# A layer of state space and attention: tables stored in eight parts, attention loads held back by the emitter, its clock corrected, and one vector operation exchanged

## The chip, the cores and the metric

One core of a Trainium2 chip. The metric is the device time of one execution in microseconds (us). The kernel before was timed three times: 1916.57, 1918.79 and 1922.06 us, median 1918.79. A separate, profiled execution left the trace that all rows below come from. TensorE is called PE, VectorE DVE, ScalarE ACT, GpSimd POOL, SyncE SP.

## The reference

S = 2048 tokens, D = 1024 channels, one layer, fp32. In short:

```python
mod = silu(c) @ w_ada + b_ada                       # shift | scale | gate
u = layer_norm(h) * (1 + scale) + shift
(x_ssm, z_ssm, q, k, v, f_logit, z_attn, g_ssm, g_attn) = split(u @ w_in)
y_ssm = s5(x_ssm)                # 32 groups of 16 channels, 64 complex states, scan over 2048 tokens, gelu, GLU
y_ssm = (y_ssm * silu(z_ssm)) @ w_proj_ssm
log_f = log_sigmoid(f_logit + b_f)
# 8 heads of 64: causal softmax(q k / 8 + cum_f[t] - cum_f[j]) @ v
y_attn = (o * silu(z_attn)) @ w_proj_attn
merged = sigmoid(g_ssm) * y_ssm + sigmoid(g_attn) * y_attn
h = layer_norm(ALPHA * h + (merged @ w_out) * gate, ln_g, ln_b)
```

## The kernel before, in words

**Products.** Each fp32 matrix is split into a high and a low part, and a product is the sum of three matmuls (high·high, low·high, high·low). A tile of the input projection (`pp` in the rows) is 8 times three matmuls of 128x512 in one of four PSUM banks. `uh`/`ul` are the parts of the modulated input, `hi`/`lo` those of the weights, loaded as `raw` and split on POOL.

**Stages in order of time.** The modulation sums `acc` over eight chunks of `w_ada` on DVE, and PE sums them over partitions (`bg<-ident,acc`, with `pr` for the keys' weights); x is normalized on DVE and transposed on PE (`pt<-ident,xt`); the projection follows, whose results go through `st` to scratch in HBM (`x_sc`, `zs_sc`, `q_sc`, `k_sc`, `ga_sc`, ...). Beside it, DVE computes the state-space tables `pk` (128 x 32 groups x 163 numbers), which SP writes to `pk_sc`. The 32 state-space groups come next, still beside projection tiles: `stage_l` (L988) loads `pkg` (one group's table) and `xr`, POOL builds `G` and others, DVE builds `CA`, and `bg<-CA,pkg` is the first matmul of a group. Then attention: 64 rounds (8 heads, 8 pairs of query blocks) of scores (`sc<-ks,qd`), exponentials (`srow`), their transposes (`pt<-ident,srow`) and products with v (`acc`), with the GLU and the two projections (`bg<-bh,wh` and the like) put between. `ks`, `fb`, `vs` are a chunk of 512 keys, biases and values; `qd` the queries of two rounds. `lb` is four divided by a row's sum of exponentials, spread over 64 columns, which PE transposes (`acc<-ident,lb`). The output projection and the last layer norm end the program.

**Order of the work.** Nothing reorders instructions on the chip. `Model` (L42) is a rough clock: `cost` (L99) gives each instruction's duration, `deps` (L80) when its operands are there. `merge` (L168) takes streams in order of rank and emits the next step of the first one that would not wait at the model's PE time; so the numbers in `cost` decide what stands where on every engine. `Engine` calls go through L209, which is why nearly all rows say L209. `sp.dma_start` puts a transfer into SP's single queue at once; `sp.later` (L223) holds it until the model says that its operands are there. SP works in order: a transfer that waits holds up those behind it. The two merges are at L663 (start) and L1760 (the rest). `pools` (L1230) opens the room of attention in two steps, `at["p"]` when the state space is done, `atp` when the projection is done; a ring of six chunks has two places in the first and four in the second.

The lines that matter most:

```python
# L105, cost, PE
return max(n, 2) * (0.4167 if n >= 256 else 1.667)
# L963, ssm_params
sp.dma_start(out=pk_sc.rearrange("g p n -> p g n"), in_=pk)
# L1583, exponentials
dve.tensor_scalar(out=lb, in0=li.to_broadcast([128, 2, 64]), scalar1=4.0, scalar2=None, op0=ALU.mult)
```

Of the kernel before, what the change touches and what calls it, by code (L numbers as in the profile page):

```python
# [16 lines left out]
S = 2048  # L17
D = 1024
NW = 4          # token windows of 512
WT = 512  # L20
KD = D // 128
NG = 32         # state-space groups
GH = 16         # channels of a group
CL = 8          # tokens of a chunk
NCH = S // CL   # chunks
CW = WT // CL   # chunks of a window
# [10 lines left out]
PKN = 163       # of a group: Bbar 16 | swapped 16 | C 16 | swapped 16 | tables 64 | powers 19 | A^7..A^0 16  # L37
# [4 lines left out]
class Model:  # L42
    """A rough clock of the engines, by which the order of emission is chosen (it computes no data)."""

    # from the end of an instruction to the start, on another engine (or the same), of one that needs it
# [34 lines left out]
    def deps(self, e, kw):  # L80
        """When the operands are there for engine e (whose own accesses are in order)."""
        rd, wt = self.aps(kw)
        r = 0.0
        for n in rd:
            if n in self.wr:
                end, by = self.wr[n]
                r = max(r, end + self.lat(e, by))
            for h in self.held:
                if n in h[2]:           # (a transfer that is still to come)
                    r = max(r, max(h[0] + 1100, self.t["sp"] + 1100, self.t["dma"]) + 1700)  # L90
# [8 lines left out]
    def cost(self, e, op, kw):  # L99
# [4 lines left out]
        if e == "pe":  # L104
            if op == "transpose":  # L105
                return n * 0.835
            if kw["rhs"].dtype == F32R:
                return max(n, 2) * (0.4167 if n >= 256 else 1.667)
            return max(n * 1.667, 60.0)
# [12 lines left out]
        if e == "act":  # L122
            c = (60 if kw["in_"].space == PSUM else 95) + 0.833 * n
            return c + 178 * isinstance(kw.get("scale"), bass.AP) + 90 * ("accum_out" in kw)
        if e == "pool":
            if op == "memset":
# [4 lines left out]
                   and v.space == bass.MemoryType.DRAM and v.ap[-1][0] == 1] + [512])  # L131
        return n * o.shape[0] * 4 / 360.0 * 512 / row

    def run(self, e, op, kw):
        c, r = self.cost(e, op, kw), self.deps(e, kw)
        if e == "sp":
# [3 lines left out]
            end = self.t["dma"] + 1000  # L140
# [5 lines left out]
        for n in wt:  # L146
            # parts of a tile that transfers fill do not wait for each other
# [3 lines left out]
    def settle(self, rd, wt, dma=False):  # L151
        """Emit what is held and has to come before a read of rd and a write of wt (transfers may fill parts of a
        tile in any order)."""
# [14 lines left out]
    def merge(self, streams):  # L168
        """Emit from the first stream whose next step would not wait; streams come in order of rank."""
# [27 lines left out]
class Engine:  # L197
    """An engine whose instructions the model sees."""
# [14 lines left out]
    def when(self, **kw):  # L213
        """When an instruction with these operands could start."""
# [3 lines left out]
    def soon(self, op, /, **kw):  # L218
        """A stream's step: the instruction, emitted once it would not wait."""
# [3 lines left out]
    def later(self, op, /, **kw):  # L223
        """The instruction, emitted once its operands are there (the streams go on meanwhile)."""
# [6 lines left out]
def hybrid_layer(ctx: ExitStack, tc: tile.TileContext, x, c, w_ada, b_ada, w_in, b_f, lam_re, lam_im,  # L231
# [32 lines left out]
    def pround(o, i):  # L264
        """Pool's copy into float32r (its rounding)."""
# [13 lines left out]
    bt = const.tile([128, 24], F32, name="bt")  # L279
    psp = pl(ctx, "psp", space=PSUM)  # L280
# [4 lines left out]
    # maskb[q, k] = 0 where k <= q, NEG elsewhere  # L285
# [4 lines left out]
    # ------------------------------------------------------------------ phase 1: input projection  # L290
    esl = ExitStack()               # left: until the projection is done
# [11 lines left out]
    def ps_tile(n=[0]):  # L303
        """One of four banks, which attention later has for scores (three) and outputs."""
# [7 lines left out]
    def bg_tile(n=None):  # L312
        if n is not None and n % 4 > 1:         # (the banks of the transposes, once attention is done)
            return pt_tile()
# [5 lines left out]
    def bank():  # L320
        """Whichever of the two banks of bg_tile is free."""
# [12 lines left out]
    def split_wide(raw, n):  # L334
        """A stream that splits a chunk of weights; the tiles are there at once."""
# [8 lines left out]
    def rstd_of(p, mv, n):  # L344
        """1 / sqrt(var + eps) of the variances mv[:, :, 1]."""
# [21 lines left out]
    def until(f):  # L367
        """A condition to wait on, whatever the time."""
        return lambda: 0.0 if f() else None

    def modulation():
        """shift | 1 + scale of silu(c) @ w_ada + b_ada, as columns, 128 channels at a time."""
# [3 lines left out]
        act.activation(out=one, in_=ident[:, 0:1], func=AF.Sqrt)    # (its table is there when the layer norm needs it)  # L376
# [43 lines left out]
    def early_keys():  # L420
        """Two column tiles of the keys' weights, with which the first window goes on while the next one comes."""
# [7 lines left out]
    def modulation_columns():  # L429
        """Sums over the partitions, as columns."""  # L430
# [17 lines left out]
    def column_sums(acc, n, c0):  # L448
        """mods[:, c0:] = sums of acc over its partitions, as columns, + b_ada."""
# [34 lines left out]
    def normalized():  # L484
        """Windows of tokens, less their mean and over their spread."""
# [21 lines left out]
    def modulated():  # L507
        """u = normalized * (1 + scale) + shift, channels on partitions."""
# [28 lines left out]
    def low_parts():  # L537
        """The two parts of u."""
# [23 lines left out]
    def products_of(ps, w, hi, lo, c0):  # L562
        """A tile of columns of the projection of a window."""
# [7 lines left out]
    def store_parts(kind, m, w, ps):  # L571
        """Queries (scaled) or keys, in two parts."""
# [92 lines left out]
    # the other columns, with the state-space branch alongside  # L665
# [55 lines left out]
    def forget_bias():  # L721
        """f_sc[h, t] = cumulative log_sigmoid(f + b_f)."""
        with ExitStack() as es:
# [10 lines left out]
            # log1p(e) = 2 artanh(s), s = e / (2 + e) <= 1/3  # L734
# [25 lines left out]
    def gate():  # L760
        """The gate part of the modulation, as a row (scaled by 1/16, which the merge leaves)."""
# [1029 lines left out]
```

## Time and profile before

| | |
|---|---|
| median of three executions | 1918.79 us |
| span of the profiled execution | 1913.3 us |
| PE busy | 1833.8 us (96%), 10104 matmuls |
| DVE busy | 1082.5 us (57%) |
| POOL busy | 923.6 us (48%) |
| ACT busy | 775.1 us (41%) |
| moved by DMA | 252.37 MB, mean 132 GB/s |

The span is the time from the first to the last instruction of the profiled execution; the median execution is 5.5 us longer, which is what lies around the span and the difference between executions. The shares are averages over stages that differ: POOL is busy 48% over the span and 94% in the state-space groups. What a row calls a wait is idle time of an engine, put down to what ended it.

### The profile page before, as it was taken

The numbers are of one execution on the slowest core, as the hardware profiler recorded it, in microseconds if no ns is written. First come the engines' busy times: TensorE is split into PE (matmuls) and PEld (weight loads), VectorE is DVE, ScalarE is ACT, GpSimd is POOL, SyncE is SP. The second block draws the span as 40 slices with busy tenths as digits, with TensorE's granted clock in tenths as the row PEclk, the third lists the DMA queues.
The fourth block names the chain that finished last, engine by engine and source line by source line (L and its number), as shares of the span: only waits on it lengthen the run. The fifth ranks groups of instructions, "written<-read, shape, count | busy, mean of one in ns | idle before, by whom it ended". The sixth has DMA issues, their size and how long they took to land. (4 is left out here: it accounts for less than half of the span.)

```text
span 1913.3 us, 30538 instructions
## 1 busy us (share of the span) xinstructions
PE 1833.8 (96%) x10104; PEld 1565.5 (82%) x10104; DVE 1082.5 (57%) x2886; ACT 775.1 (41%) x1849; POOL 923.6 (48%) x1343
## 2 busy tenths in 40 slices
PE   4999999998999999999998999999999999899997
PEld 3789988886787888888887888988889888788886
DVE  8651114734555555552004777876777866567666
ACT  5441111121433444443114767876767866311110
POOL 5222111113889999995306566376543436533110
PEclk9899999998999999999998999999999999999999
DMA  9434346654333333335217365265364543744432
GB/s 302 138 86 119 94 110 183 149 133 121 101 94 105 100 105 97 105 101 138 91 50 189 98 169 140 77 183 152 113 201 131 151 137 127 260 146 136 131 123 89
DMA packets 276915, 252.37 MB, mean 132 GB/s; under 512 B 66396, under 2 KB 211828, under 8 KB 276756
## 3 DMA queue, kind: packets, MB, share of 16 engines
q1 hardware_dynamic: 276756, 250.41, 45.7%
q8 instruction: 80, 1.31, 0.3%
q14 instruction: 79, 0.65, 0.1%
HBM read 159.50 MB, written 86.63 MB: 129 GB/s over the span
## 5 line engine op out<-in xcount | busy, mean ns | idle before, releaser
L209 PE MATMUL pp<-uh,hi 128*128 128x512 f32 x1136 | 451.0, 397 | 0.0
L209 PE MATMUL pp<-uh,lo 128*128 128x512 f32 x1136 | 446.0, 393 | 0.0
L209 PE MATMUL pp<-ul,hi 128*128 128x512 f32 x1136 | 445.1, 392 | 0.0
L209 ACT ACTIVATE st<-pp 128x512 f32<-128x512 f32 (+2 forms) x168 | 93.9, 559 | 439.1 <-PE pp L209 383.4
L209 DVE TENSOR_TENSOR pl<-pt,ph 128x512 fp32r<-128x512 f32 (+1 forms) x288 | 183.3, 657 | 122.3 <-ACT ph L209 121.7
L209 PEld LDWEIGHTS pp<-uh,lo 128*128 128x128 f32 x1136 | 214.2, 189 | 46.3
L209 PEld LDWEIGHTS pp<-uh,hi 128*128 128x128 f32 x1136 | 216.4, 190 | 41.5
L209 PEld LDWEIGHTS pp<-ul,hi 128*128 128x128 f32 x1136 | 214.7, 189 | 41.9
L209 ACT ACTIVATE srow<-srow,nm 128x512 f32<-128x512 f32 (+2 forms) x320 | 207.6, 653 | 0.4 <-DVE nm L209 0.3
L209 ACT ACTIVATE ph<-pt 128x512 fp32r<-128x512 f32 (+1 forms) x288 | 159.8, 572 | 64.4 <-PE pt L209 51.6
L209 DVE CUSTOM_DVE_ANT_0 srow<-sc,fb 128x512 f32<-128x512 f32 (+3 forms) x288 | 163.0, 594 | 21.9 <-PE sc L209 21.9
L209 PE MATMUL sc<-ks,qd 128*128 128x512 f32 (+2 forms) x640 | 163.7, 381 | 7.1 <-DMA qd<-q_sc 7.1
L209 PE MATMUL pt<-ident,srow 128*128 128x128 f32 x1088 | 159.3, 275 | 8.7 <-DVE pl L209 4.7
L209 PE MATMUL acc<-ph,vs 128*128 128x256 f32 x576 | 163.0, 308 | 2.5 <-POOL ph L209 2.5
L209 POOL TENSOR_TENSOR oo<-oo 64x256 f32<-64x256 f32 x128 | 93.7, 732 | 143.0 <-ACT oo L209 140.0
L209 POOL TENSOR_SCALAR hi<-raw 128x512 fp32r<-128x512 f32 x60 | 39.9, 665 | 237.8 <-PE pp L209 191.7
L209 PEld LDWEIGHTS pt<-ident,srow 128*128 128x128 f32 x1088 | 128.4, 141 | 27.2 <-DVE pl L209 9.5
L209 PE MATMUL acc<-pl,vs 128*128 128x256 f32 x576 | 147.4, 282 | 0.5 <-DVE pl L209 0.5
L209 PE MATMUL bg<-bh,wh 128*128 128x512 f32 (+1 forms) x384 | 140.2, 365 | 5.1 <-DVE zt L209 5.1
L209 PE MATMUL bg<-bh,wl 128*128 128x512 f32 (+1 forms) x384 | 138.1, 360 | 0.0
L209 PE MATMUL bg<-bl,wh 128*128 128x512 f32 (+1 forms) x384 | 137.8, 359 | 0.0
L209 PEld LDWEIGHTS sc<-ks,qd 128*128 128x128 f32 x640 | 107.9, 193 | 24.4 <-issue 8.4
(240 smaller groups left out, 3811.3 us busy)
## 6 DMA issues: line engine op xcount, KB each, us to landing
xt<-in_x_dram SPq DMA_DIRECT2D x32, 512.0 KB, 3.7
qd<-q_sc SPq DMA_DIRECT2D x64, 256.0 KB, 5.4
raw<-in_w_in_dram SPq DMA_DIRECT2D x30, 512.0 KB, 4.5
wada<-in_w_ada_dram SPq DMA_DIRECT2D x16, 512.0 KB, 7.0
k_sc<-st SPq DMA_DIRECT2D x32, 256.0 KB, 3.3
v_sc<-st SPq DMA_DIRECT2D x32, 256.0 KB, 2.3
q_sc<-st SPq DMA_DIRECT2D x16, 512.0 KB, 3.3
gs_sc<-st SPq DMA_DIRECT2D x32, 256.0 KB, 2.3
```

The source lines that it names most:

```text
L209: return fn(kw["out"], 0.0) if op == "memset" else fn(**kw)
```

## The change

- **The clock** (`Model.cost` and `run`): a matmul of 256 columns or more costs 13 ns more; an activation that also sums costs 185 ns for it instead of 90; a transfer's duration follows another formula in the length of its rows; a transfer ends 1600 ns instead of 1000 after its data.
- **The tables**: `pk` is stored in eight transfers of four groups each. `stage_l` loads a group once the clock says that its own part is stored.
- **The attention loads** (`load_keys`, `load_q`) are held back (`sp.later`) instead of being put into SP's queue at once, and `pools` asks for one more `load_q` and two more `load_keys` as soon as `atp` is open.
- **lb**: a product with a constant tile of fours instead of a product with the number 4.

The rest of the diff removes comments. Its core:

```diff
@@ Model.cost, Model.run
-                return max(n, 2) * (0.4167 if n >= 256 else 1.667)
+                return 13 + 0.4167 * n if n >= 256 else max(n, 2) * 1.667
...
-            return c + 178 * isinstance(kw.get("scale"), bass.AP) + 90 * ("accum_out" in kw)
+            return c + 178 * isinstance(kw.get("scale"), bass.AP) + 185 * ("accum_out" in kw)
...
-                   and v.space == bass.MemoryType.DRAM and v.ap[-1][0] == 1] + [512])
-        return n * o.shape[0] * 4 / 360.0 * 512 / row
+                   and v.space == bass.MemoryType.DRAM and v.ap[-1][0] == 1] + [4096])
+        return n * o.shape[0] * 4 / row * (9 + 0.045 * row) / 16
...
-            end = self.t["dma"] + 1000
+            end = self.t["dma"] + 1600
@@ hybrid_layer
+    fours = const.tile([128, 2, 1], F32, name="fours")
...
+    nc.gpsimd.memset(fours, 4.0)
@@ ssm_params, stage_l
             yield sp.when(in_=pk)
-            sp.dma_start(out=pk_sc.rearrange("g p n -> p g n"), in_=pk)
+            for i in range(0, NG, PKG):
+                sp.dma_start(out=pk_sc[i:i + PKG].rearrange("g p n -> p g n"), in_=pk[:, i:i + PKG])
+                sq["stored"].append(M.t["dma"] + 2500)
...
+    PKG = 4
...
-            yield sp.when(out=pk, b=xr)
+            yield max(sp.when(out=pk, b=xr), sq["stored"][g // PKG])
+            M.t["sp"] = max(M.t["sp"], sq["stored"][g // PKG])
             sp.dma_start(out=pk, in_=pk_sc[g])
@@ load_keys, load_q (the other four transfers likewise)
-        sp.dma_start(out=f32(ks), in_=k_sc[h, :, :, tk].rearrange("a d t -> (a d) t"))
+        sp.later("dma_start", out=f32(ks), in_=k_sc[h, :, :, tk].rearrange("a d t -> (a d) t"))
@@ pools
         atp = pl(esat, "atp", side="right")
+        load_q()
+        load_keys()
+        load_keys()
@@ exponentials
-                dve.tensor_scalar(out=lb, in0=li.to_broadcast([128, 2, 64]), scalar1=4.0, scalar2=None, op0=ALU.mult)
+                dve.tensor_mul(out=lb, in0=li.to_broadcast([128, 2, 64]), in1=fours.to_broadcast([128, 2, 64]))
```

What it moves, in the program's own order. PE at the start, from the end of the second of the eight column sums (a sum is two of `bg<-ident,acc` and two of `bg<-ident,pr`) to the first projection matmuls; before:

```order
L209 MATMUL bg<-ident,acc 128x128
L209 MATMUL bg<-ident,pr 128x128
L209 MATMUL pt<-ident,xt 128x128 x8
L209 MATMUL bg<-ident,acc 128x128
L209 MATMUL bg<-ident,pr 128x128
L209 MATMUL bg<-ident,acc 128x128
L209 MATMUL bg<-ident,pr 128x128
L209 MATMUL pp<-uh_0_84,hi 128x512
L209 MATMUL pp<-ul_0_100,hi 128x512
L209 MATMUL pp<-uh_0_84,lo 128x512
L209 MATMUL pp<-uh_0_84,hi 128x512
L209 MATMUL pp<-ul_0_100,hi 128x512
```

Now:

```order
L209 MATMUL bg<-ident,acc 128x128
L209 MATMUL bg<-ident,pr 128x128
L209 MATMUL bg<-ident,acc 128x128
L209 MATMUL bg<-ident,pr 128x128
L209 MATMUL pp<-uh_0_86,hi 128x512
L209 MATMUL pp<-ul_0_102,hi 128x512
L209 MATMUL pp<-uh_0_86,lo 128x512
L209 MATMUL pp<-uh_0_86,hi 128x512
L209 MATMUL pp<-ul_0_102,hi 128x512
L209 MATMUL pp<-uh_0_86,lo 128x512
L209 MATMUL pt<-ident,xt 128x128 x4
L209 MATMUL pp<-uh_0_86,hi 128x512
```

Eight transposes of x stood behind the second sum, and the projection began behind the third. Now four transposes stand ahead of the second sum, and the projection begins behind it. Ahead of the eighth sum stand 22 triples of projection matmuls instead of 12.

SP where the state-space tables are stored (`pk_sc<-pk`) and the first groups loaded (`pkg`, `xr`); before:

```order
L209 DMA zs_sc<-st 128x512 x3
L209 DMA raw<-in_w_in_dram 128x8x128
L209 DMA pk_sc<-pk 128x32x163
L209 DMA dsk<-in_ssm_d_dram 16x32x1
L209 DMA pkg<-pk_sc 128x163
L209 DMA xr<-x_sc 128x256
L209 DMA pkg<-pk_sc 128x163
L209 DMA xr<-x_sc 128x256
L209 DMA zs_sc<-st 128x512 x3
```

Now:

```order
L209 DMA zs_sc<-st 128x512 x2
L209 DMA pk_sc<-pk 128x4x163 x8
L209 DMA dsk<-in_ssm_d_dram 16x32x1
L209 DMA zs_sc<-st 128x512
L209 DMA pkg<-pk_sc 128x163
L209 DMA xr<-x_sc 128x256
L209 DMA pkg<-pk_sc 128x163
L209 DMA xr<-x_sc 128x256
L209 DMA raw<-in_w_in_dram 128x8x128
```

One store became eight, one projection store now stands ahead of the first `pkg`, and a load of weights went from ahead of the tables to behind the second group. On PE the first `bg<-CA,pkg` stands behind 2053 projection matmuls instead of 2083; between the first and the last group stand 1494 instead of 1509.

SP where the projection ends and attention starts; before:

```order
L209 DMA ga_sc<-st 128x512 x13
L209 DMA qd<-q_sc 64x2x512 x2
L209 DMA ks<-k_sc 128x512
L209 DMA fb<-f_sc 128x512
L209 DMA vs<-v_sc 128x4x128
L209 DMA yr<-y_sc 128x8x64 x2
L209 DMA wraw<-in_w_glu_dram 128x4x128 x2
L209 DMA zt<-zs_sc 128x512 x3
L209 DMA qd<-q_sc 64x2x512 x2
```

Now:

```order
L209 DMA ga_sc<-st 128x512 x13
L209 DMA qd<-q_sc 64x2x512 x2
L209 DMA ks<-k_sc 128x512
L209 DMA fb<-f_sc 128x512
L209 DMA vs<-v_sc 128x4x128
L209 DMA ks<-k_sc 128x512
L209 DMA fb<-f_sc 128x512
L209 DMA vs<-v_sc 128x4x128
L209 DMA yr<-y_sc 128x8x64 x2
L209 DMA wraw<-in_w_glu_dram 128x4x128 x2
L209 DMA zt<-zs_sc 128x512 x3
L209 DMA qd<-q_sc 64x2x512 x2
```

A second chunk of keys (`ks`, `fb`, `vs`, 256 KB each) now stands between the first and the second pair of `qd`. At the other end of attention, nine triples of background products instead of six stand behind the last `acc` on PE.

## Rows read from the trace of the kernel before

**Rows 1.** The page: its head and part 1 (busy us, share of span, instructions).
```profile
span 1913.3 us, 30538 instructions
...
PE 1833.8 (96%) x10104; PEld 1565.5 (82%) x10104; DVE 1082.5 (57%) x2886; ACT 775.1 (41%) x1849; POOL 923.6 (48%) x1343
```
**Rows 2.** Stretches: length, busy time of each engine, TensorE's clock, DMA share, GB/s.
```profile
600.00:700.00 100.00, 100.00 (x476) 80.51 (x475) 53.67 (x117) 42.69 (x104) 93.82 (x148) 1.00 0.36 102
1050.00:1600.00 550.00, 532.54 (x3405) 469.02 (x3404) 415.87 (x1365) 394.60 (x994) 295.37 (x458) 0.99 0.49 141
1600.00:1700.00 100.00, 91.06 (x564) 82.34 (x563) 59.95 (x108) 33.44 (x72) 56.12 (x63) 0.97 0.61 200
```
**Rows 3.** Waits of PE: what for, us in total, times, longest.
```profile
PE bg L209 <- DVE acc L209: 13.7, 7, 2.8
...
PE bg L209 <- DVE CA L209: 7.6, 1, 7.6
PE sc L209 <- DMA qd<-q_sc: 7.1, 2, 6.9
PE bg L209 <- DVE zt L209: 5.1, 3, 3.8
...
PE acc L209 <- DVE lb L209: 3.1, 4, 1.4
```
**Rows 4.** Timeline of PE at the first group: start, us, instruction, [idle before].
```profile
459.52 0.39 PE L209 MATMUL pp<-uh,lo 128*128 128x512 f32 x1
467.48 0.61 PE L209 MATMUL bg<-CA,pkg 128*16 128x128 f32 x2 [7.58 <-DVE CA L209]
...
472.14 0.51 PE L209 MATMUL pp<-uh,hi 128*128 128x512 f32 x1
```
**Rows 5.** Timeline of all engines from the last table entry to CA.
```profile
444.33 0.43 DVE L209 TENSOR_TENSOR pk<-ta,ta 128x256 f32<-128x256 f32 x1
...
459.33 0.33 SPq L209 DMA_DIRECT2D pkg<-pk_sc  x1
...
461.29 0.41 POOL L209 TENSOR_TENSOR G<-pkg 128x128 f32<-128x128 f32 x1 [12.48 <-DMA pkg<-pk_sc]
...
464.10 0.60 ACT L209 ACTIVATE st<-pp 128x512 f32<-128x512 f32 x1 [13.08 <-DMA zs_sc<-st]
...
465.34 0.54 DVE L209 SCALAR_TENSOR_TENSOR CA<-pkg,sgn 128x144 f32<-128x144 f32 x1
```
**Rows 6.** The page, part 6: DMA issues, KB each, us to landing.
```profile
ks<-k_sc SPq DMA_DIRECT2D x32, 256.0 KB, 5.9
...
pk_sc<-pk SPq DMA_DIRECT2D x1, 2608.0 KB, 14.5
```
**Rows 7.** Timeline of ACT: two projection tiles in a row (24 matmuls apart).
```profile
434.11 0.60 ACT L209 ACTIVATE st<-pp 128x512 f32<-128x512 f32 x1 [4.84 <-PE pp L209]
439.55 0.60 ACT L209 ACTIVATE st<-pp 128x512 f32<-128x512 f32 x1 [4.84 <-PE pp L209]
```
**Rows 8.** Timeline of SP and PE where attention starts.
```profile
1014.34 1.27 SPq L209 DMA_DIRECT2D qd<-q_sc  x2
...
1026.69 1.26 SPq L209 DMA_DIRECT2D qd<-q_sc  x2
...
1033.67 1.62 PE L209 MATMUL sc<-ks,qd 128*128 128x512 f32 x3 [6.89 <-DMA qd<-q_sc]
```
**Rows 9.** Stretches while tables are stored and where attention starts (columns of rows 2).
```profile
446.00:458.00 12.00, 12.00 (x55) 9.94 (x54) 1.05 (x4) 0.60 (x1) 2.73 (x3) 1.00 1.09 217
...
1026.00:1032.00 6.00, 0.78 (x3) 0.30 (x2) 4.96 (x16) 4.35 (x13) 6.00 (x7) 0.73 0.89 241
```
**Rows 10.** Tile lb: ns min/median/max, first and last start.
```profile
L209 DVE TENSOR_SCALAR lb<-li x64: 226/230/2329, 1018.1 to 1607.8; 128x128 f32<-128x128 f32 x64
```
**Rows 11.** Tile m in the groups, same columns.
```profile
L209 DVE TENSOR_TENSOR m<-bg,cs x32: 405/423/426, 475.0 to 877.9; 128x256 f32<-128x256 f32 x32
...
L209 DVE TENSOR_TENSOR m<-gs,cs x32: 406/662/1341, 479.9 to 880.2; 128x255 f32<-128x255 f32 x32
```
**Rows 12.** Timeline of PE at the eighth column sum.
```profile
53.83 0.63 PE L209 MATMUL pp<-uh,lo 128*128 128x512 f32 x1
55.73 0.76 PE L209 MATMUL bg<-ident,acc 128*128 128x128 f32 x2 [1.27 <-DVE acc L209]
```
**Rows 13.** Timeline of ACT where the second window's products begin.
```profile
81.81 0.60 ACT L209 ACTIVATE st<-pp 128x512 fp32r<-128x512 f32 x1 [4.36 <-DMA x_sc<-st]
```

More of the change, by code (lines that the diff above doesn't have):

```diff
@@ L962, in ssm_params @@
             yield sp.when(in_=pk)
-            sp.dma_start(out=pk_sc.rearrange("g p n -> p g n"), in_=pk)
-    sq = dict(a=0, b=0, c=0, d=0, e=0, r=0, x=0, t=0, ready=False, st={})
+            for i in range(0, NG, PKG):
+                sp.dma_start(out=pk_sc[i:i + PKG].rearrange("g p n -> p g n"), in_=pk[:, i:i + PKG])
+                sq["stored"].append(M.t["dma"] + 2500)
+    PKG = 4
+    sq = dict(stored=[], a=0, b=0, c=0, d=0, e=0, r=0, x=0, t=0, ready=False, st={})
     esss = ExitStack()
@@ L1209, in load_keys @@
         tk = slice(j * 512, (j + 1) * 512)
-        sp.dma_start(out=f32(ks), in_=k_sc[h, :, :, tk].rearrange("a d t -> (a d) t"))
-        sp.dma_start(out=fb, in_=f_sc[h:h + 1, tk].to_broadcast([128, 512]))
-        sp.dma_start(out=f32(vs), in_=v_sc[h, tk, :].rearrange("(n p) e -> p n e", p=128))
+        sp.later("dma_start", out=f32(ks), in_=k_sc[h, :, :, tk].rearrange("a d t -> (a d) t"))
+        sp.later("dma_start", out=fb, in_=f_sc[h:h + 1, tk].to_broadcast([128, 512]))
+        sp.later("dma_start", out=f32(vs), in_=v_sc[h, tk, :].rearrange("(n p) e -> p n e", p=128))
         at["k"][h, j], at["v"][h, j], at["f"][h, j] = ks, vs, fb
@@ L1221, in load_q @@
         for hf in range(2):
-            sp.dma_start(out=f32(qd[hf * 64:(hf + 1) * 64]),
-                         in_=q_sc[:, h * 64:(h + 1) * 64, p_ * 256:(p_ + 2) * 256].rearrange("a d t -> d a t"))
+            sp.later("dma_start", out=f32(qd[hf * 64:(hf + 1) * 64]),
+                     in_=q_sc[:, h * 64:(h + 1) * 64, p_ * 256:(p_ + 2) * 256].rearrange("a d t -> d a t"))
         at["q"][r], at["q"][r + 1] = qd[:, :, 0:256], qd[:, :, 256:512]
```

## The prediction

> **What bounds the kernel now.** I read part 1 of the page first. PE is busy 1833.8 of 1913.3 us [rows 1], so all that any change of order can win is the 79.5 us in which PE stands idle, plus what PE loses by a lower clock after idling. No edit adds or removes a matmul. The second view is the list of PE's waits [rows 3]: the reader is to see that no single wait is large. The sums of the modulation cost 13.7 us in seven waits, the first state-space group 7.6 in one, the second pair of queries 7.1, the merge's operands 5.1, lb 3.1. The third view is the table of stretches [rows 2]: in the state-space groups PE is busy 100.00 of 100.00 us, and POOL beside it 93.82; in attention PE is busy 532.54 of 550, so 17.5 us are idle there, in many short gaps; in the merge 91.06 of 100. So there are four places where the change can win, and one (the groups) where it can only lose.
>
> **The change part by part.** All terms are against the profiled span of 1913.3 us. The median execution, 1918.79, is 5.5 us above that, and I carry these 5.5 us over. A difference below about 0.3% (5.8 us) can't be told from no change here.
>
> *Tables in eight parts.* The last entry of `pk` is written at 444.33 (+0.43), and the store takes 14.5 us to land [rows 5, 6]. SP waits for it, issues the first `pkg` at 459.33, POOL starts on it at 461.29, and PE's first matmul of a group starts at 467.48 after 7.58 us idle [rows 4, 5]. Part of the time behind the landing is not the tables': ACT's `st` at 464.10 waited 13.08 us for a store of projections that stood in SP's queue behind the waiting `pkg`, and DVE's `CA` (465.34) stands behind the `st` of the same tile. After the idle time PE runs at half pitch until 472.14, which costs half of 472.14 − 467.48 = 4.66, so 2.3 us. The place costs 7.6 + 2.3 = 9.9 us in all.
>
> In the new order the last entry of `pk` stands one projection tile earlier. A tile is 439.55 − 434.11 = 5.44 us [rows 7], or 226.7 ns for each of its 24 matmuls; so the tables are ready between 437 and 439.3. PE however wants the first group 30 matmuls earlier, at 459.75 − 30 × 0.2267 = 452.95 [rows 4]. When does the first `pkg` land? The stretch of the store moves 217 GB/s at a DMA share of 1.09 [rows 9], so the engines are full, and eight parts take the same 14.5 us together as the one did. If `pkg` goes ahead once its own part is written (1/8 of 14.5, 1.8 us, and 2 us for the load by 459.33 to 461.29), it is there at 441 to 443, far ahead of PE, and the whole 9.9 us go. If its packets go behind all parts, it is there at 451.5 to 453.8, `CA` takes 467.48 − 465.34 = 2.1 us more, and PE waits 0.7 to 3 us. One projection store now stands ahead of `pkg`, so that ACT's wait goes in any case. If everything stays late by what it is now, only the shift helps: 1 us. Ends −10 and −1; I take −7, nearer to the upper one, because the parts of both queues that made `CA` late are gone in every case but the last.
>
> *Start.* Before the eighth column sum PE waits for DVE's `acc` [rows 12], as before most of the eight, 13.7 us in all [rows 3]. The chain of `acc` on DVE is not touched. The new order has ten more triples of projection matmuls ahead of the eighth sum; a triple is 3 × 0.2267 = 0.68 us, so up to 6.8 us of work lie in time that was idle. All of it counts only if what follows can use it: the products of the second window have to wait for transposes and low parts, and ACT's `st` there waited 4.36 us for a store [rows 13], so PE may only come to the next wait earlier. Ends −6 (nearly all kept) and +2 (projection matmuls that now stand ahead of a sum hold that sum up, where their own operands are late); I take −3.
>
> *Attention loads.* At the transition PE waits 6.89 us for the second pair of queries, issued at 1026.69, 12.35 us after the first pair [rows 8]. In the new order three more transfers of 256 KB stand between them, an extra `ks`, `fb` and `vs`. At 241 GB/s in that stretch, with a DMA share of 0.89 [rows 9], 768 KB take 3.2 us. The work on PE before these scores is the same, so the wait grows to about 10 us. Against that, the chunk of keys is there earlier for a later round, where no wait is seen now. A held-back transfer is also let into the queue no later than the model thinks that its room is free, so that SP's queue stands still less; ends 0 and +6 (twice the extra, if the landing of a transfer stretches from 5.9 us [rows 6] in the crowd). I take +3.
>
> *lb.* 64 instructions of median 230 ns and at most 2329 [rows 10]: the long ones are long beside POOL's work, and PE waits 3.1 us for them in all [rows 3]. A product of two tensors of this size should be 250 to 300 ns: `m<-bg,cs` does 256 elements in 423, half of that and some fixed part. If it isn't stretched, up to 3 us of waits go; if each of the 64 takes 50 ns more, that is 3.2 us on DVE, of which PE sees a part, since it waits for `lb` in 4 rounds of 64; +1 is the upper end. I take −1. What the row of `m` shows: the same product with one operand in PSUM has a median of 423 ns, with both in SBUF 662 and a longest of 1341 [rows 11]; and both operands of the new `lb` are in SBUF.
>
> The Trainium skill ("SBUF — State Buffer", section "Who interferes with whom") says that DVE and GpSimd share a pair of ports under an exclusive lock, and it counts a product of two tensors that are both in SBUF among the operations that take it; by that the exchange of the operation buys nothing. The trace agrees in the 662 ns. By that rule this term would be 0 and the sum 1 us higher.
>
> *The clock of the emitter, in groups and attention.* A matmul of 512 columns now counts 226.3 ns (13 + 213.3), which is what the trace shows [rows 7], instead of 213.3. An order made by a PE clock that runs 6% fast gives operands 6% more time on the chip than the model thinks; that cushion goes. In the groups PE can't get better than 100% busy [rows 2]; in attention, with 17.5 us idle, a truer clock of ACT's sums may close some gaps. From −6 (a third of the gaps) to +12 (half of rival A below). I take 0: the number of projection matmuls among the groups, 1494 instead of 1509, has hardly moved.
>
> *Merge.* Nine triples of background products instead of six stand behind the last `acc` of attention, 3 × 0.68 = 2 us more cover for waits of 5.1 us for `zt` [rows 3]. Ends −3 and +1; −2.
>
> Sum: −7 − 3 + 3 − 1 + 0 − 2 = −10. Span 1903.3, time 1903.3 + 5.5 = 1909 us.
>
> **The rivals.**
>
> *A, slower: the lost cushion.* Place: the 32 groups, 468 to 890, 13.2 us each. The old clock gave 13.3 ns a matmul, 6% of 422 us or 25 us in all, 0.78 us a group. If POOL's or DVE's part of each group now arrives late by most of that, PE idles 0.75 us × 32 = 24 us, and the rest of the sum stays: 1918.8 − 10 + 24 = 1933. It decides the sign from 0.5 us a group (16 us) on. For it: POOL is busy 93.82 of 100 [rows 2], so there is little room in which a late POOL catches up. Against it: PE has no wait at all there, and the order of POOL's work hardly changes.
>
> *B, no change: the eight parts bring nothing.* `pkg`'s packets line up behind the seven other parts, SP's later transfers behind its wait, and `CA` stays late; the term is −1 instead of −7, the sum −4: 1915. For it: DMA is full during the store, share 1.09 [rows 9]. Against it: SP's queue now holds a projection store ahead of the wait. The Trainium skill ("DMA: Bandwidth & Descriptors", the part on HWDGE ordering) says that each DMA engine takes descriptors in the order of its ring. By that the first `pkg` would land behind all eight parts; the trace of before has one store alone and does not show it.
>
> *C, more: attention's gaps close too.* A third to a half of the 17.5 us [rows 2], −8 on top: 1901. For it: the sums on ACT were counted 95 ns too short, if the new number is right. Against: DVE with 415.87 and ACT with 394.60 of 550 are both near what they can do when each waits for the other.
>
> **How the numbers follow.** Forecast 0.5, A 0.2, B 0.2, C 0.1. The forecast's own range is −16 to −4, so 1903 to 1915. Faster than 1913.0: 0.42 of the forecast's 0.5, all of C, 0.06 of B: 0.58. Slower than 1924.5: 0.17 of A, 0.02 of the rest: 0.19. Within: 0.23. The range, 1898 to 1924, has B, C and the forecast whole, and leaves out A.
>
> **What would show it.** Tables: the wait before the first `bg<-CA,pkg` is below 3 us, and ACT's `st` there doesn't wait 13. Start: the waits for `acc` sum to less than 9 us, and the first `st` of the second window comes some 3 us earlier. Loads: the wait for the second `qd` is 8 to 13 us. Clock: stretches 600 to 700 stay at 100 busy; a PE there below 97 is rival A. lb: waits for it below 3 us. What would make it wrong is above all waits of PE for `CA`, `G` or the scan's tiles inside the groups, or many new short waits in attention for `pl`, `ph` and `srow`.

## The result and the profile after

The changed kernel takes 1937.22 us (median of 4 runs, 1936.33 to 1939.78) against 1919.56 for the kernel before in the same comparison: ratio 1.010, 95% interval 1.008 to 1.012. It is 18 us slower, where 10 us faster was forecast. Rival A, the lost cushion, had named 1933. In all comparisons below one execution alone, of e4, fell into a slower state (2402 us), and e4's time is the median of its other three.

The page of the changed kernel, head and part 1:

```profile
span 1935.1 us, 30547 instructions
...
PE 1837.8 (95%) x10104; PEld 1559.8 (81%) x10104; DVE 1085.0 (56%) x2886; ACT 773.4 (40%) x1849; POOL 929.2 (48%) x1344
```

The work is the same as in [rows 1]; PE's idle time went from 79.5 to 1935.1 − 1837.8 = 97.3 us. The stretches (length, busy time of PE, weight loads, DVE, ACT and POOL, clock, DMA share, GB/s) say where:

```profile
500.00:600.00 100.00, 97.37 (x458) 78.14 (x457) 57.07 (x119) 38.71 (x94) 88.59 (x140) 1.00 0.35 95
600.00:700.00 100.00, 97.19 (x458) 77.07 (x457) 55.96 (x114) 41.36 (x103) 91.57 (x147) 1.00 0.35 99
700.00:800.00 100.00, 96.87 (x451) 76.75 (x449) 47.77 (x104) 38.98 (x97) 87.86 (x146) 1.00 0.34 97
800.00:900.00 100.00, 95.95 (x446) 76.82 (x445) 35.70 (x84) 35.09 (x86) 70.44 (x111) 1.00 0.40 109
...
1050.00:1600.00 550.00, 530.11 (x3361) 463.37 (x3362) 409.35 (x1340) 389.70 (x978) 295.84 (x455) 0.99 0.51 141
```

The groups, in which PE was busy 100.00 of 100 us from 600 to 700 [rows 2], now have it busy for 96 to 97, with the clock at 1.00. PE's waits (what for, us in total, times, longest) name what is late there:

```profile
PE sc L209 <- DMA qd<-q_sc: 10.2, 2, 9.9
PE pt L209 <- DVE pl L209: 8.3, 9, 3.4
PE bg L209 <- POOL xl L209: 6.7, 7, 1.1
PE bg L209 <- DVE CA L209: 6.0, 1, 6.0
PE bg L209 <- DVE zt L209: 5.2, 1, 5.2
PE bg L209 <- DVE acc L209: 5.2, 3, 2.8
PE bg L209 <- ACT T L209: 5.0, 4, 1.9
...
PE acc L209 <- DVE lb L209: 1.3, 3, 0.6
```

`xl` and `T`, the operands of a group's matmuls, stood in no wait of note before (`T` 0.5 us, `xl` none). The wait for `acc` fell from 13.7 to 5.2 us, that for `CA` only from 7.6 to 6.0, that for `qd` rose from 7.1 to 10.2 [rows 3].

To compare orders that differ, I gave every matmul of a trace the median distance to the next matmul that those of its shape and tiles have in the kernel before, summed these to a measure of work, and took the time at which a given amount of work has started, less that work: the time lost so far. Its growth, by stretches of work (us; all from the profiled executions):

```
work, us             0-200  200-400  400-480  480-920  920-1040  1040-1600  lost in all
what it holds        start  project. tables   groups   transit.  attention
kernel before         21.7    1.3     11.3      6.4     14.0      44.4       112.4
changed               18.2    1.3     12.0     22.5     16.2      49.5       133.1
e1 PE's old number    14.9    1.3      6.5      6.5     16.9      51.2       110.5
e2 PE's number alone  20.3    8.1     15.4     23.0     14.9      55.5       151.0
e3 DVE, POOL longer   19.4    1.3      8.3      5.5     16.1      49.3       113.2
e4 old transfers      18.8    8.4     14.0     22.5     18.6      55.9       151.1
e5 e1, old loads      15.0    1.3      4.5      6.7     17.5      51.2       109.4
e6 e1, old lb         14.8    1.3      5.2      6.7     16.9      54.0       112.3
e7 eight parts alone  21.6    1.3      9.3      5.4     15.2      45.2       111.3
e8 e1, first ahead    15.8    1.4     15.2      5.4     15.5      53.6       120.3
e9 e1, ACT's old no.  16.2    1.3      4.3      6.7     16.3      47.9       106.1
e10 e1, first merge   15.2    1.3      8.9      5.4     15.2      55.7       115.0
e11 e10, old loads    15.4    1.3      8.5      5.4     15.1      56.3       115.3
e12 ACT's no. alone   20.4    1.3     11.6      7.2     15.1      48.4       117.5
```

The last column also holds what is lost before the first matmul (13 us) and behind attention (0.3), but not the 10 to 11 us from the last matmul to the end. The figures in the expectations of e3 and e5 are of earlier forms of this measure and lie some us higher; e10's count the first 13 us in. The border between transition and attention is rough: by shape alone, without the tiles, the kernel before has 18.6 and 40.4 there and the changed one 16.8 and 49.4, while the groups differ by 16 all the same. Executions of one kernel differ by some us, so a difference of 2 us in this table is no finding; 16 us in the groups is one.

### The profile page after: what moved, and what is told of

Read it like the earlier page. It is cut to its first block, busy times and chain, and to the rows that moved or that the text cites. A ratio compares the mean times of both kernels' runs of the same rounds, so it can differ in the third digit from the quotient of the medians.

```text
span 1935.1 us, 30547 instructions
## 1 busy us (share of the span) xinstructions
PE 1837.8 (95%) x10104; PEld 1559.8 (81%) x10104; DVE 1085.0 (56%) x2886; ACT 773.4 (40%) x1849; POOL 929.2 (48%) x1344
## 5 line engine op out<-in xcount | busy, mean ns | idle before, releaser
L209 PE MATMUL pp<-uh,hi 128*128 128x512 f32 x1136 | 451.5, 397 | 0.1
L209 PE MATMUL pp<-ul,hi 128*128 128x512 f32 x1136 | 445.1, 392 | 5.6 <-POOL ul L209 3.4
L209 PE MATMUL pp<-uh,lo 128*128 128x512 f32 x1136 | 444.9, 392 | 0.0
L209 ACT ACTIVATE st<-pp 128x512 f32<-128x512 f32 (+2 forms) x168 | 94.2, 561 | 436.4 <-PE pp L209 377.4
L209 PEld LDWEIGHTS pp<-ul,hi 128*128 128x128 f32 x1136 | 214.4, 189 | 49.9 <-POOL ul L209 5.6
L209 PEld LDWEIGHTS pp<-uh,lo 128*128 128x128 f32 x1136 | 213.9, 188 | 46.4
L209 PEld LDWEIGHTS pp<-uh,hi 128*128 128x128 f32 x1136 | 216.0, 190 | 42.1 <-ACT uh L209 0.8
L209 DVE TENSOR_TENSOR pl<-pt,ph 128x512 fp32r<-128x512 f32 (+1 forms) x288 | 183.9, 657 | 112.5 <-ACT ph L209 110.0
L209 ACT ACTIVATE srow<-srow,nm 128x512 f32<-128x512 f32 (+2 forms) x320 | 207.8, 654 | 1.2 <-DVE nm L209 1.1
L209 ACT ACTIVATE ph<-pt 128x512 fp32r<-128x512 f32 (+1 forms) x288 | 160.3, 572 | 81.3 <-PE pt L209 69.3
L209 DVE CUSTOM_DVE_ANT_0 srow<-sc,fb 128x512 f32<-128x512 f32 (+3 forms) x288 | 163.8, 595 | 21.1 <-PE sc L209 20.6
L209 PE MATMUL sc<-ks,qd 128*128 128x512 f32 (+2 forms) x640 | 163.1, 378 | 12.3 <-DMA qd<-q_sc 10.2
L209 PE MATMUL pt<-ident,srow 128*128 128x128 f32 x1088 | 159.8, 275 | 13.5 <-DVE pl L209 8.3
L209 PE MATMUL acc<-ph,vs 128*128 128x256 f32 x576 | 163.8, 309 | 0.0
L209 POOL TENSOR_SCALAR hi<-raw 128x512 fp32r<-128x512 f32 x60 | 40.0, 667 | 245.9 <-PE pp L209 181.4
L209 PEld LDWEIGHTS pt<-ident,srow 128*128 128x128 f32 x1088 | 127.2, 141 | 35.4 <-DVE pl L209 18.4
L209 POOL TENSOR_TENSOR oo<-oo 64x256 f32<-64x256 f32 x128 | 93.8, 733 | 123.4 <-ACT oo L209 120.6
L209 PE MATMUL acc<-pl,vs 128*128 128x256 f32 x576 | 148.5, 284 | 0.3 <-DVE pl L209 0.2
L209 PE MATMUL bg<-bh,wh 128*128 128x512 f32 (+1 forms) x384 | 139.6, 364 | 8.4 <-DVE zt L209 5.2
L209 PE MATMUL bg<-bl,wh 128*128 128x512 f32 (+1 forms) x384 | 137.9, 359 | 0.0
L209 PE MATMUL bg<-bh,wl 128*128 128x512 f32 (+1 forms) x384 | 137.7, 358 | 0.0
L209 PEld LDWEIGHTS sc<-ks,qd 128*128 128x128 f32 x640 | 106.3, 191 | 28.7 <-issue 11.1
```

Source lines behind the costliest of these rows:

```text
L209: return fn(kw["out"], 0.0) if op == "memset" else fn(**kw)
```

## The experiments

The theory after the result: the old clock gave a matmul of 512 columns 213.3 ns where the chip takes 226.7 [rows 7]. That error made up for others of the same sign: DVE's and POOL's instructions in the groups are counted too short as well. With PE alone corrected, the order puts group matmuls at places where the model has their operands ready and the chip has not. Rivals: the transfers' new times, the held loads.

**e1, PE's old number in the changed kernel.**

```diff
-                return 13 + 0.4167 * n if n >= 256 else max(n, 2) * 1.667
+                return max(n, 2) * (0.4167 if n >= 256 else 1.667)
```

> The changed kernel with one number of the emitter's clock put back: a matmul of 512 columns counts 213.3 ns again instead of 226.3. Theory (lost cushion): the time lost in the state-space groups falls from 18 us more than in the kernel before to about none, PE in stretches 600 to 700 and 700 to 800 is busy above 99 of 100, and the time falls by 12 to 20 us, to 1917 to 1925. Rival (the transfers' new times or the groups' held loads made the groups late): it stays at 1934 to 1940, and PE waits for xl and T as now.

1910.94 us, ratio to the kernel before 0.9961 (0.9946 to 0.9976): 26 us less than the changed kernel, more than the 12 to 20 expected. The groups lose 6.5 us as before. Stretches and PE's waits from 470 to 880:

```profile
600.00:700.00 100.00, 100.00 (x477) 80.42 (x476) 55.41 (x115) 41.83 (x102) 92.33 (x152) 1.00 0.37 104
700.00:800.00 100.00, 100.00 (x474) 80.17 (x473) 56.88 (x110) 41.82 (x103) 91.73 (x148) 1.00 0.37 102
```

```profile
PE bg L209 <- DVE sl L209: 0.2, 1, 0.2
```

One line of the emitter's clock, which the chip never executes, fills PE again while POOL is as busy as before. The rest of the change with this line undone is faster than the kernel before by 0.4%.

**e2, PE's number alone in the kernel before.** The same line, the other way round.

> The kernel before with that one number alone changed (13 ns more for a matmul of 256 columns or more), all else as before. Theory (lost cushion): slower by 12 to 25 us, 1931 to 1945, with waits of PE for POOL's and ACT's tiles inside the groups and PE at 95 to 98 of 100 there. Rival (other parts of the change): 1917 to 1922.

1953.76 us, ratio 1.018 (1.016 to 1.020): 36 us slower, outside the expected range. The groups lose 23.0 us, and other stretches lose more than before too: 7 us in the projection ahead of the tables, 4 in the tables, 11 in attention. Stretches of this run:

```profile
600.00:700.00 100.00, 96.27 (x450) 75.65 (x449) 52.59 (x114) 40.68 (x101) 89.15 (x143) 1.00 0.36 103
...
1050.00:1600.00 550.00, 518.28 (x3266) 451.63 (x3266) 402.65 (x1320) 383.56 (x961) 295.05 (x448) 0.98 0.52 142
```

So the number costs more by itself than in the change: the change's other numbers soften it.

**e3, DVE and POOL counted as the trace has them, in the groups.** The rows of the changed kernel in the groups (count, busy us, mean ns, idle before):

```profile
L209 DVE TENSOR_TENSOR_SCAN gs<-pkg,m 128x256 f32<-128x256 f32 x27 | 28.4, 1052 | 17.0 <-POOL m L209 17.0
L209 DVE TENSOR_TENSOR m<-gs,cs 128x255 f32<-128x255 f32 x27 | 16.9, 627 | 0.8
...
L209 DVE TENSOR_TENSOR CA<-CA,t 128x144 f32<-128x144 f32 x27 | 14.1, 523 | 0.9
```

```profile
L209 POOL TENSOR_TENSOR sw<-sw,sn 128x256 f32<-128x256 f32 x27 | 20.4, 756 | 7.6 <-ACT sw L209 7.6
```

The model has 68 + 1.042 × 256 = 335 ns for the scan and nearly that for `m`, 218 for `CA`, 130 + 2.14 × 256 = 678 for `sw`. A row's time is not all the engine's: the next instruction can start before it ends, 0.08 us on DVE (`m<-bg,cs`, 0.42 us from 700.30, the next at 700.64) and 0.05 here on POOL, where 0.69 us lie between two starts:

```profile
701.55 0.74 POOL L209 TENSOR_TENSOR m<-m,sw 128x256 f32<-128x256 f32 x1
702.24 0.52 POOL L209 TENSOR_TENSOR G<-G,t 128x128 f32<-128x128 f32 x1
```

So the model's 678 ns for POOL is nearly right, and the 70 ns that this run adds there are more of a margin than a correction. For DVE the difference is far larger than this overlap.

```diff
+            if self.grp and op == "tensor_tensor_scan":
+                return 1050
+            if self.grp and 128 <= n and all(v.space != PSUM for v in ins):
+                c += 250
...
+            if self.grp:          # POOL
+                c += 70
```

> The changed kernel, in whose clock also DVE and POOL are counted, in the state-space groups, as the trace shows them: a scan 1050 ns, a DVE instruction of 128 or more elements with all operands in SBUF 250 ns more, a POOL instruction 70 ns more. Theory (the fast PE clock made up for DVE and POOL being counted too short): the groups lose less than 10 us instead of 26, and the time falls by 10 to 18 us, to 1919 to 1927. Rival (any order made with the exact PE clock loses here, as POOL is the bound): the groups lose 20 us or more, 1933 or more.

1917.0 us, ratio 0.9992 (0.9978 to 1.0006): 20 us less than the changed kernel, with PE's exact number kept. The groups lose 5.5 us, and of PE's waits from 470 to 880 this is left (L216 is the line that is L209 elsewhere):

```profile
PE bg L216 <- DVE il L216: 0.2, 1, 0.2
```

This is the run that carries the theory: the exact PE number doesn't hurt by itself, but beside DVE and POOL costs that leave too little time. Between the first and the last group now stand 1596 projection matmuls, against 1494 in the changed kernel and 1506 in e1. DVE's error alone (the changed kernel) is worse than both errors together (e1); PE's error alone, the old number beside the longer DVE and POOL, was not run. Nor were DVE and POOL tried apart, or the same time added elsewhere, so that it is DVE's true cost and not just any margin that helps is argued from the rows, not shown. And e3 only comes back to the time before: e1, with the wrong number, is 6 us faster.

**e4, the transfers' old times in the changed kernel.**

```diff
-                   and v.space == bass.MemoryType.DRAM and v.ap[-1][0] == 1] + [4096])
-        return n * o.shape[0] * 4 / row * (9 + 0.045 * row) / 16
+                   and v.space == bass.MemoryType.DRAM and v.ap[-1][0] == 1] + [512])
+        return n * o.shape[0] * 4 / 360.0 * 512 / row
...
-            end = self.t["dma"] + 1600
+            end = self.t["dma"] + 1000
```

> The changed kernel with the transfers' old times in the clock (old formula, 1000 ns at the end). Theory (PE's number alone costs the cushion; the transfers' times gave the 3 us at the start): the start's gain goes and the groups stay as bad, 1937 to 1943. Rival (the transfers' longer times made the groups late): the groups lose less than 12 us, 1920 to 1926.

1953.76 us, ratio 1.0185 (1.0162 to 1.0207). The groups stay as bad (22.5), so the rival falls; but the run is 17 us slower than the changed kernel, more than the 6 expected at most. The table has it: 7 us in the projection (8.4 instead of 1.3), 6 in attention, 2 each at tables and transition. The start's gain, which was to go, stays (18.8, against 18.2). With the exact PE number the longer transfers are worth 17 us.

**e5, the attention loads undone, on e1.** `sp.dma_start` again for the five transfers, and the three extra calls in `pools` gone.

> Base: the changed kernel with PE's old number (1910.9 us). Here the attention loads are put back too: into SP's queue at once, and no extra query and key loads when attention's room opens. Theory (the extra key chunk delays the second pair of queries, as forecast): the wait for qd falls from about 10 to 7 us and the time by 2 to 4 us, to 1907 to 1909; the attention stage, which loses 54 us with the base and 47 in the kernel before, stays at 52 or more, since it is the order by the transfers' and ACT's new costs that loses there. Rival (the held loads themselves open gaps in attention): attention's loss goes back to 47 to 49 us and the time falls by 6 to 9 us, to 1902 to 1905.

1912.49 us, ratio 0.9973 (0.9958 to 0.9988), which can't be told from e1. The wait for `qd` is 3.5 us instead of e1's 9.1, and what that wins is lost in attention's next rounds: between 1000 and 1200 PE waits 11.1 us for `pl`, against 4.8 in e1. PE's waits of e1, then of e5:

```profile
PE sc L209 <- DMA qd<-q_sc: 9.1, 2, 7.9
PE pt L209 <- DVE pl L209: 7.6, 7, 2.8
```

```profile
PE pt L209 <- DVE pl L209: 13.8, 8, 3.3
...
PE sc L209 <- DMA qd<-q_sc: 3.5, 2, 2.6
```

Both expected times miss: the held loads are worth nothing that shows, and attention's extra loss of 7 us on this base (51.2 against 44.4) isn't theirs.

**e6, the old lb, on e1.**

```diff
-                dve.tensor_mul(out=lb, in0=li.to_broadcast([128, 2, 64]), in1=fours.to_broadcast([128, 2, 64]))
+                dve.tensor_scalar(out=lb, in0=li.to_broadcast([128, 2, 64]), scalar1=4.0, scalar2=None, op0=ALU.mult)
```

> The same base with lb as a product with the number 4, as before. Theory (forecast: the exchange brings about 1 us): 1910 to 1914, with lb at a longest of over 1.5 us again. Rival (a product of two tensors in SBUF is held up by POOL just as much): no difference, within 2 us of 1911, and the longest lb of the changed kernel is as long as before.

1916.7 us, ratio 0.9997 (0.9982 to 1.0012). That is 5.8 us more than e1 by medians from two comparisons, outside both expectations, though the profiled spans differ by 1.8 us (1913.6 and 1911.8). The tile's rows (ns min/median/max) in the changed kernel and in e6:

```profile
L209 DVE TENSOR_TENSOR lb<-li,fours x64: 291/293/2004, 1030.0 to 1628.1; 128x128 f32<-128x128 f32 x64
```

```profile
L209 DVE TENSOR_SCALAR lb<-li x64: 226/300/2914, 1005.5 to 1613.4; 128x128 f32<-128x128 f32 x64
```

The longest is as long with either operation. Between 1050 and 1600 the mean is 494 ns before and 493 ns in the changed kernel, and over all 64 it is 500 and 535, so no gain in DVE's time shows. As the model counts the new operation longer (201 ns against 137), the order in attention shifts, and whether that is worth the 2 to 6 us stays open.

**e7, the eight parts alone in the kernel before.**

> The kernel before with the tables stored in eight parts and nothing else changed. Forecast's term: the wait for CA falls from 7.6 us to below 3, and the time by 5 to 9 us, to 1909 to 1913. Rival (the first pkg lands behind all eight parts): the wait stays at 5 to 8 us, the time at 1915 to 1919.

1912.57 us, ratio 0.9975 (0.9961 to 0.9989): faster by 5 us, in the range of the forecast's term, but not by its mechanism, so that the time is luck. The wait for `CA` is 6.8 us instead of 7.6 and the tables' stretch loses 9.3 instead of 11.3; the rest of the 5 us is spread or within what executions differ by (the profiled spans differ by 1.1).

**e8, the first two groups' loads ahead of the other seven parts, on e1.**

```diff
                 sq["stored"].append(M.t["dma"] + 2500)
+                if i == 0:
+                    for g in range(2):
...
+                        sp.dma_start(out=t0, in_=pk_sc[g])
+                        sp.dma_start(out=t1, in_=x_sc[g * GH:(g + 1) * GH].rearrange("h j c -> (h j) c"))
```

> Base: the changed kernel with PE's old number (1910.9 us). Here the loads of the first two groups (tables and inputs) stand in SP's queue right behind the first of the eight parts, ahead of the other seven. If pkg was late because it lined up behind seven parts: it lands within 6 us of the first part's issue, the wait for CA (2.9 us in the base, 6.0 in the changed kernel) is gone or below 1 us, and the time falls by 2 to 5 us, to 1906 to 1909. Rival (DVE's and ACT's work ahead of CA, which waits for stores of projections, makes CA late): POOL has the tables early but PE's wait for CA stays at 3 us or more, and the time stays at 1909 to 1913.

In the changed kernel, the tables' timeline (start, us, instruction, idle before):

```profile
434.61 7.50 SPq L209 DMA_DIRECT2D pk_sc<-pk  x8
...
445.13 0.43 SPq L209 DMA_DIRECT2D pkg<-pk_sc  x1
...
451.49 2.86 SPq L209 DMA_DIRECT2D zs_sc<-st  x2
452.69 0.60 ACT L209 ACTIVATE st<-pp 128x512 f32<-128x512 f32 x1 [10.48 <-DMA zs_sc<-st]
452.90 0.42 POOL L209 TENSOR_TENSOR G<-pkg 128x128 f32<-128x128 f32 x1 [7.51 <-DMA pkg<-pk_sc]
...
453.92 0.46 DVE L209 SCALAR_TENSOR_TENSOR CA<-pkg,sgn 128x144 f32<-128x144 f32 x1
```

The eight parts are issued by 442.1, `pkg` at 445.13, and its data is there only at 452.9, 7.8 us later. Then PE's first matmul of a group:

```profile
455.72 0.61 PE L209 MATMUL bg<-CA,pkg 128*16 128x128 f32 x2 [6.00 <-DVE CA L209]
```

In e8, the same place:

```profile
433.62 0.37 SPq L209 DMA_DIRECT2D pk_sc<-pk  x1
...
437.08 0.32 SPq L209 DMA_DIRECT2D pkf<-pk_sc  x1
...
438.87 6.18 SPq L209 DMA_DIRECT2D pk_sc<-pk  x7
...
439.06 0.42 POOL L209 TENSOR_TENSOR G<-pkf 128x128 f32<-128x128 f32 x1 [17.14 <-DMA pkf<-pk_sc]
...
455.25 0.28 DVE L209 COPY kd<-bg 16x128 f32<-16x128 f32 x1 [14.04 <-DMA zs_sc<-st]
455.28 0.62 POOL L209 TENSOR_TENSOR tta<-pkf 128x256 f32<-128x256 f32 x1 [14.19 <-DMA zs_sc<-st]
...
455.52 0.60 ACT L209 ACTIVATE st<-pp 128x512 f32<-128x512 f32 x1 [13.57 <-DMA zs_sc<-st]
```

Issued ahead of the other seven parts, which follow from 438.87 on, the load (here `pkf`) lands in 2.0 us (437.08 to 439.06). So it was late because it stood behind the parts, and that much is shown. But the time is 1915.46 us, ratio 0.9997 (0.9983 to 1.0011), 4.5 us more than e1 by the medians: now DVE, POOL and ACT all stop until 455.3 for transfers behind the seven parts, and PE waits 5.0 us for `il` and 5.6 for `xl` instead of 2.9 for `CA`. Both theories were half right: the wait was taken away and came back one step later, since the other seven parts still pass ahead of everything that follows.

**e9, ACT's old number, on e1.**

```diff
-            return c + 178 * isinstance(kw.get("scale"), bass.AP) + 185 * ("accum_out" in kw)
+            return c + 178 * isinstance(kw.get("scale"), bass.AP) + 90 * ("accum_out" in kw)
```

> Base: the changed kernel with PE's old number (1910.9 us). Here ACT's summing activation counts 90 ns again instead of 185. From work unit 1040 us to 1600 us the kernel before loses 44.4 us, the base 51.1. If ACT's new number makes attention worse, that goes back to 46 or less and the time falls by 4 to 7 us, to 1904 to 1907. Rival (the transfers' new times do it): 50 to 53 us lost, 1909 to 1913.

1908.31 us, ratio 0.9952 (0.9937 to 0.9968), the lowest time of all that ran, though by the ratios it can't be told from e1 (0.9961). Attention loses 47.9 us instead of 51.2, between what the theory and the rival expected.

**e10, the transfers' new times in the first merge only, on e1; e11, the old attention loads on top.** A flag in the model, put down after the first merge, chooses between the two formulas.

> The same base; here the transfers' new times hold only until the program's first merge is done (start and first window of the projection), the old ones after it. If the transfers' new times win 7 us at the start and lose 6 in attention: the start's gain stays (28 us lost at work unit 200 against 34.8 before), attention loses 44 to 47, and the time falls to 1903 to 1907. Rival (ACT's number or the held loads make attention worse): attention stays at 50 or more, 1909 to 1913.

> As the run before, and the attention loads put back into SP's queue at once, without the extra ones. If the held loads cost what the wait for the second pair of queries shows (9.1 us with them, 3.5 without, on the base), it is 2 to 5 us faster than the run before. Rival (what is won at that wait is lost again in attention's next rounds, as on the base): within 2 us of it.

1915.05 us, ratio 0.9996 (0.9985 to 1.0007), and 1916.56, ratio 1.0004 (0.9994 to 1.0015). Both are 0.35% or more behind e1 (0.9961), and outside the expected times. The start's gain stays (15.2 lost), but attention loses 55.7 and 56.3: my theory that the transfers' new times cost attention falls. With ACT's new number they help there (51.2 against 55.7). The old loads again change nothing.

**e12, ACT's number alone in the kernel before.**

> The kernel before with ACT's summing activation counted 185 ns instead of 90, and nothing else. If this number makes attention worse by itself (55.7 us lost between work units 1040 and 1600 with it and the transfers' old times, 44.4 in the kernel before): attention loses 50 to 57, the rest is as before, 1921 to 1929. Rival (it is the mixture with the other edits): attention stays at 43 to 47, 1915 to 1920.

1924.37 us, ratio 1.0039 (1.0023 to 1.0056): slower by 7 us by this ratio and 6 by the medians, as the theory has it, with 48.4 us lost in the attention stretch, short of the 50 expected; the wait for `pl` there grew to 10.5 us. So this number, too, costs by itself. It is not wrong: the rows of the changed kernel's attention are

```profile
L209 ACT ACTIVATE srow<-srow,nm 128x512 f32<-128x512 f32 x205 | 146.6, 718 | 0.0
...
L209 ACT ACTIVATION_READ_ACCUMULATOR srow<-srow,nm 128x1 f32 x291 | 56.7, 195 | 0.0
```

and a timeline of ACT there shows what a sum adds:

```profile
1300.78 0.71 ACT L209 ACTIVATE srow<-srow,nm 128x512 f32<-128x512 f32 x1
1301.39 0.19 ACT L209 ACTIVATION_READ_ACCUMULATOR srow<-srow,nm 128x1 f32 x1
1301.48 0.58 ACT L209 ACTIVATE ph<-pt 128x512 fp32r<-128x512 f32 x1
```

From the exponential to the next instruction are 0.70 us, and with the new number the model counts 95 + 0.833 × 512 + 185 = 706 ns. DVE's `pl` has a mean of 687 ns where the model has 68 + 1.042 × 512 = 602, but this is the overlap again: two of them in a row take 1.20 us from start to next start.

```profile
1310.72 1.29 DVE L209 TENSOR_TENSOR pl<-pt,ph 128x512 fp32r<-128x512 f32 x2 [1.92 <-ACT ph L209]
1311.92 0.68 DVE L209 CUSTOM_DVE_ANT_0 srow<-sc,fb 128x512 f32<-128x512 f32 x1
```

So e3's reason, DVE counted too short, does not carry over to `pl`, and why ACT's right number costs in attention stays open.

## Why the prediction was wrong

- **The step that failed** is "The clock of the emitter, in groups and attention", taken at 0 with a range of −6 to +12. It measured +16.1 in the groups (6.4 to 22.5) and +5.1 in attention (44.4 to 49.5), 21 of the 32 us by which the span missed (1935.1 against 1903.3); the tables are 8 more. The groups' part is PE's number: e1 takes it out, e2 brings it alone. Attention's part stays open: beside the change's other numbers PE's makes little difference there (51.2 in e1, 49.5 with it), alone it costs 11 us (e2), and ACT's alone 4 (e12). I took the unmoved count of projection matmuls among the groups (1494 instead of 1509) as a sign that nothing changed. The count is not the place: the same number of matmuls in front of operands that are late is a wait, and an order shows no lateness.
- **Rival A** had the mechanism, the place and nearly the size: 0.50 us a group instead of 0.75 (16.1 / 32). That its 1933 came so near is in part luck: it kept −10 for the other terms, where about +6 came, and had +24 in the groups, where 16 came. I gave it 0.2 because PE showed no wait in the groups. But a stretch at 100.00 busy can only lose, and POOL at 93.82 was the row to weigh. What A lacked is the reason why the cushion was needed: DVE's scan takes about three times what the model counts (rows of e3).
- **Start**, −3: measured 18.2 instead of 21.7, so −3.5. The waits for `acc` follow the transfers' new times: 5.2 us with them, 12.7 in e4 and 13.5 in e7 without. The loss of the stretch does not follow so simply: with PE's old number the new times are worth 6 us or more (14.9 in e1, 15.2 in e10, 21.6 in e7), with the exact one 0.6 (18.2, and 18.8 in e4). So the number came out, and how is in part open.
- **Tables**, −7: +0.7 in the changed kernel (11.3 to 12.0). PE was ready for the first group at 455.72 − 6.00 = 449.72, 3.2 us ahead of the 452.95 of the working, which had left out that what the start wins makes PE come earlier here; nor did its second case count the load's own time behind the parts. ACT's wait for a store, which was to go in any case, was still 10.48 us. With PE's old number the first group stands 36 projection matmuls later (e1's trace), and the stretch loses 5 to 7 us less than before with the transfers' new times (e1, e5, e6, e9), 2 to 3 without them (e7, e10, e11). The second of my two cases for `pkg`, behind all parts, is the one that holds (e8). The Trainium skill ("DMA: Bandwidth & Descriptors", on HWDGE ordering) says that each DMA engine takes the descriptors of a ring in order; the 7.8 us behind the parts and the 2.0 ahead of them agree with it.
- **Attention loads**, +3: the wait grew by the 3 us forecast, 6.89 to 9.94, and the stretch by 2.2. The row of after that answers to [rows 8]:

```profile
1049.78 0.77 PE L209 MATMUL sc<-ks,qd 128*128 128x512 f32 x1 [9.94 <-DMA qd<-q_sc]
```

  That it is worth 3 us was wrong: e5 and e11 take it away and gain nothing.
- **lb**, −1: 0 in the operation's time between 1050 and 1600 (494 and 493 ns), though its median, 293 ns, lies in the 250 to 300 of the working; the long ones stayed. PE's waits for it fell from 3.1 to 1.3 us in the changed kernel, but are 3.7 in e1. The rule that the prediction cites from the Trainium skill ("SBUF — State Buffer", "Who interferes with whom") gave 0, and 494 and 493 ns agree. What the new order that comes with it is worth stays open (e6).
- **Merge**, −2: within 1 us of nothing; the waits for `zt` are 5.2 and 3.3 us, against 5.1 and 3.9 before.
- **Offset**, 5.5 us: the changed kernel's runs lie 1.8 us above their spans. The profile of before was of an execution some us faster than the median, which is why the spans differ by 21.8 us and the medians by 18.

## What to carry to other kernels

A hand-made clock that orders instructions is tuned as a whole: correct one engine's number and the errors of the others, which it had hidden, become waits. Correct all engines that meet at a wait, or leave a margin, and judge each number by a run of its own; here that brought back 20 of the 26 us that the correction had cost (e3). Read such numbers from start to start of instructions in a row, since their records overlap. A stage at 100% busy has nothing to win from a truer order, so ask first what keeps it full. Terms that stand one behind the other are not independent: what is won ahead of a wait can be lost at it. And cutting a store into parts brings the first part's reader forward only if that read is issued ahead of the other parts; even then whatever stands behind them waits.

## What was not expected of the hardware

A load of 81.5 KB landed 2.0 us after its issue ahead of seven stores of 326 KB, and 7.8 us after it behind eight (e8 and the changed kernel). In the groups the scan of 256 elements on DVE took 1052 ns on average, `m` and `CA` with all operands in SBUF 627 and 523, 1.9 and 2.4 times what the model's formula gives, beside a POOL that was busy 88 to 92 of 100 us; no run took POOL's work away, so that POOL stretches them is not shown.
